# Expert gates: one-hot matrices of eight tokens by wide 16-bit tensor compares in place of one scalar compare per token

## The chip, the cores and the metric

One core of a Trainium2 chip runs the whole program. The metric is the device time of one launch in microseconds; the median of the runs shown is compared. PE is TensorE, PEld its weight loads, DVE is VectorE, ACT is ScalarE, POOL is GpSimd, SP the queue that issues the DMAs.

## The reference

Two stacked models of two layers each run over 256 tokens of width 1024. The change lies in the first model's expert layer, which both of its layers run:

```python
def peer_ffn(h, w_query, sub_keys, expert_u, expert_v):
    ...
    best_s, best_pos = lax.top_k(cand_s, PEER_TOPK)      # 8 heads, 16 experts of 16384 each
    idx = jnp.take_along_axis(cand_i, best_pos, axis=-1) # idx = i * 128 + j
    gate = jax.nn.softmax(best_s, axis=-1)
    ...
        act = jax.nn.gelu(jnp.einsum('cd,ced->ce', xc, u).astype(jnp.float32), approximate=False)
        return jnp.einsum('ce,ced->cd', (gc * act).astype(v.dtype), v)
```

Each token thus has 128 chosen experts, each with a gate, and its output is the sum over them of gate times gelu(x u) times v.

## The kernel before

The kernel gathers no expert. `peer` computes gelu(x u) for all 16384 experts and all tokens, and multiplies it by a dense matrix of gates that is zero where an expert wasn't chosen. The experts go in 128 chunks of 128: `uchunk(i)` takes a chunk of `uT` (512 KB by DMA), which `units` splits into a high and a low part (`whi` on ACT, L70; `wlo` by a subtraction on DVE, L74), and `sproj` forms x u by 24 matmuls of 256 columns (L96 to L98) into a PSUM bank of tag `f`. ACT applies gelu into the tile X (L451, L454). Three raw, three high and three low tiles let the loads run ahead; their instructions have a high priority.

The chosen experts come from `route(t)` on DVE (top-k, L459 to L500), which runs beside the first chunks. `softmax` is placed behind chunk EXP_AT and `slots` behind chunk IJ_AT; `slots` transposes the two halves i and j of each expert number and the gates, so that the 128 slots of a token lie on the partitions and the tokens along the free dimension (tiles IT, JT, WT).

`gates(tb, done)` then treats eight tokens at a time, 32 blocks per layer, one block behind every second chunk from GATE_AT on. For each token DVE compares the row 0 to 127 with the token's column of JT (tile B, one instruction, L531) and with its column of IT, times the gate's high and low 16-bit parts (tile A, two instructions, L533). PE multiplies B by both A's (L538, two matmuls of 128 columns per token), which sums over the slots into a 128 x 128 matrix of gates [j, i] per token, four tokens to a PSUM bank. For chunks that are already there, DVE multiplies X by the matrix (L545); for the later ones ACT copies it into X (L547), and the chunk's gelu goes to `gtmp` and is multiplied in by DVE (L452). Behind chunk 127, X is multiplied with the expert rows v (L109 to L113).

A scheduler orders each engine's instructions at build time by program order, priority and its own estimate of times; an engine then runs its list in order.

Of the kernel before, what the change touches and what calls it, by code (L numbers as in the profile page):

```python
# [12 lines left out]
F16 = mybir.dt.float16  # L13
# [3 lines left out]
ALU = mybir.AluOpType  # L17
# [4 lines left out]
S = 256  # L22
# [4 lines left out]
NEG = -1e30  # L27

PRIO = 1000
EXP_AT, IJ_AT, GATE_AT = 46, 52, 54  # L30
LN_PLAN = [(0, 1)] * 4 + [(0, 0), (1, 0), (0, 0), (0, 0), (1, 0), (0, 0)]
GSCALE = 32768.0
NCAND = [16 // (a + 1) for a in range(16)]
# [3 lines left out]
class Builder:  # L37
# [340 lines left out]
    def peer(self, l):  # L378
        nc, I, tc = self.nc, self.I, self.tc
# [2 lines left out]
        PX = px.enter_context(mk("px"))  # L382
        T = self.maker(PX)
        X = [T([128, 64, S], "X0"), None]
        io128 = T([128, 128], "io128", F16)
        nc.sync.dma_start(io128, I["c_io128"])
        JT = T([128, S], "JT")
        IT = T([128, S], "IT")
        WT = T([128, 2, S], "WT")
        T = self.maker(pr.enter_context(mk("pr", "right")))  # L390
        io50 = T([128, NC50], "io50")
        nc.sync.dma_start(io50, I["c_io50"])
# [18 lines left out]
        for t, p in enumerate(self.mblock(units)):  # L411
            q = T([128, 512], "qtok", bufs=2)
            nc.scalar.activation(q, p, AF.Copy)
            p = self.bank("t")
# [4 lines left out]
            p = self.bank()  # L419
# [6 lines left out]
        for hp, u in enumerate(units, 4):  # L426
            sk = sks[hp // 8]
            p = self.bank("f")
# [82 lines left out]
        def slots():  # L511

            for t in range(2):
                p = self.bank()
                for k in range(3):
                    tc.keep_in_program_order(nc.tensor.transpose(p[:, k * 128:(k + 1) * 128], ijws[t][:, k], self.ident))
                ts = slice(t * 128, (t + 1) * 128)
                nc.vector.tensor_copy(IT[:, ts], p[:, 0:128])
                nc.vector.tensor_copy(JT[:, ts], p[:, 128:256])
                nc.vector.tensor_scalar(WT[:, 0, ts], p[:, 256:384], GSCALE, None, ALU.mult)  # L520
                wh = T([128, 128], "wh16", F16, bufs=2)
                nc.vector.tensor_copy(wh, WT[:, 0, ts])
                nc.vector.tensor_sub(WT[:, 1, ts], WT[:, 0, ts], wh)

        def gates(tb, done):

            B = TG([128, 8, 128], "B", F16, bufs=2)
            A = TG([128, 8, 2, 128], "A", F16, bufs=2)
            for t in range(8):
                n = slice(tb * 8 + t, tb * 8 + t + 1)  # L530
                nc.vector.tensor_scalar(B[:, t], io128, JT[:, n], None, ALU.is_equal)  # L531
                for k in range(2):
                    nc.vector.tensor_scalar(A[:, t, k], io128, IT[:, n], WT[:, k, n], ALU.is_equal, ALU.mult)  # L533
            for q in range(2):
                p = self.bank("st"[q]).rearrange("p (t i) -> p t i", t=4)
                for t in range(4):
                    for k in range(2):
                        nc.tensor.matmul(p[:, t], B[:, q * 4 + t], A[:, q * 4 + t, k], start=(k == 0), stop=(k == 1))  # L538
                pv = p.rearrange("p t i -> p i t")
                ts = slice(tb * 8 + q * 4, tb * 8 + q * 4 + 4)  # L540
                for half in range(2):
                    n = min(max(done - half * 64, 0), 64)
                    o = half * 64
                    if n:
                        nc.vector.scalar_tensor_tensor(X[half][:, :n, ts], pv[:, o:o + n], 1.0 / GSCALE, X[half][:, :n, ts], ALU.mult, ALU.mult)  # L545
                    if n < 64:
                        nc.scalar.activation(X[half][:, n:, ts], pv[:, o + n:o + 64], AF.Copy, scale=1.0 / GSCALE)  # L547
            gated[0] = tb * 8 + 8
# [4 lines left out]
        for i in range(128):  # L553
            uchunk(i)
            if i == EXP_AT:
                softmax()
            if i == IJ_AT:
                slots()
                pr.close()
                X[1] = self.maker(p1.enter_context(mk("px1", "right")))([128, 64, S], "X1")  # L560
                TG = self.maker(pg.enter_context(mk("pg")))
            tb = (i - GATE_AT) // 2
            if i >= GATE_AT and (i - GATE_AT) % 2 == 0 and tb < 32:
                gates(tb, i + 1)
        pg.close()
        T = self.maker(px.enter_context(mk("pv")))
# [25 lines left out]
        T = self.maker(PL)  # L592
# [535 lines left out]
def pack_s(W):  # L1128
    d, c = W.shape
    return np.ascontiguousarray(W.reshape(d // 128, 128, c // 128, 128).transpose(2, 1, 0, 3)).reshape(c // 128, 128, d)  # L1130


def pack_m(W):
    r, c = W.shape
    q = 1024 // c
    return np.ascontiguousarray(W.reshape(r // (128 * q), q, 128, c).transpose(0, 2, 1, 3)).reshape(r // (128 * q), 128, 1024)
# [6 lines left out]
def bc(v):  # L1143
    return np.ascontiguousarray(np.broadcast_to(v, (128,) + v.shape))


def layout1(inp):
    A = {}
    x = inp["x"][0]
    A["xT"] = np.ascontiguousarray(x.T.reshape(8, 128, S).transpose(1, 0, 2))  # L1150
    A["x_tok"] = np.ascontiguousarray(x.reshape(2, 128, D).transpose(1, 0, 2))
    w = inp["w_in"]
    st = lambda f, *a: np.stack([f(*[v[l] for v in a]) for l in range(DEPTH)])

    def win(w):
        dq, dk, dv, sq, sk, sv = np.split(w, 6, axis=1)
        return np.concatenate([pack_m(dv), pack_s(np.concatenate([dq, dk, sq, sk], 1)), pack_m(sv)], 0)
    A["w_in"] = st(win, w)
    A["w_o"] = st(pack_m, inp["w_o"])
    A["w_query"] = st(pack_ms, inp["w_query"])  # L1160
    A["uT"] = st(lambda u: pack_s(u.T), inp["expert_u"])
    A["v"] = st(pack_m, inp["expert_v"])
    sk = inp["sub_keys"].reshape(DEPTH, 16, 128, 128)
    A["sub_keysT"] = np.ascontiguousarray(sk.reshape(DEPTH, 2, 8, 128, 128).transpose(0, 1, 4, 2, 3)).reshape(DEPTH, 2, 128, 1024)
    lam = np.stack([inp["lam_q1"], inp["lam_k1"], inp["lam_q2"], inp["lam_k2"]], 1)
    A["lam"] = np.ascontiguousarray(np.broadcast_to(lam[:, None], (DEPTH, 128, 4, 64)))
    A["subln_g"] = np.ascontiguousarray(np.broadcast_to(inp["subln_g"][:, None], (DEPTH, 128, 128)))
    gb = [(inp[f"ln{i}_g"][l], inp[f"ln{i}_b"][l]) for l in range(DEPTH) for i in (1, 2)]
    gb += [(inp["ln_g_2"][l, i], inp["ln_b_2"][l, i]) for l in range(DEPTH) for i in range(3)]
    gb = np.stack([np.stack(p) for p in gb])  # L1170
    A["ln_gb"] = np.ascontiguousarray(np.broadcast_to(gb[:, None], (10, 128, 2, D)))
    A["c_ident"] = np.eye(128, dtype=np.float32)
    q = np.arange(128)[:, None]
    s = np.arange(256)[None]
    dist = (128 + q - s).astype(np.float32)
    slopes = np.array([2.0 ** (-8.0 * (i + 1) / 4) for i in range(4)], np.float32)
    A["c_alibi"] = np.ascontiguousarray(np.where(dist[:, None] >= 0, -slopes[None, :, None] * dist[:, None], np.float32(NEG)).astype(np.float32))
    strict = (dist > 0).astype(np.float32)
    A["c_strict"] = np.ascontiguousarray(np.stack([strict, 1 - strict], 1))
    A["c_io128"] = bc(np.arange(128, dtype=np.float32)).astype(np.float16)  # L1180
    A["c_io50"] = bc(np.arange(NC50, dtype=np.float32))
    return A

# [97 lines left out]
```

## Time and profile before

| what | value |
|---|---|
| runs | 2992.4, 2996.71, 3002.91 us; median 2996.71 |
| profiled execution, its own time | 2998.15 us |
| its span, first to last instruction | 2996.3 us |
| mean granted TensorE clock, share of full speed | 0.983 |
| engine busy, share of the span | PE 96%, DVE 73%, ACT 49%, POOL 6% |

The profiled execution lies 1.4 us above the median. A timeline row tells an instruction's duration; instructions of one engine overlap at their ends, so what one costs its engine is read from the start of one to the start of the next. In a name, a digit at the end is left out: `io` is the tile io128 (or io50).

### The profile page before, as it was taken

Reading aid. Unit: us, or ns where it says so; the run is one execution under the profiler, and the core shown is the slowest. Engines: PE = TensorE matmul, PEld = TensorE weight load, DVE = VectorE, ACT = ScalarE, POOL = GpSimd, SP = SyncE. Lnnn points to the kernel's source line nnn. Section 1 sums busy time; section 2 is a strip of 40 time slices with the busy share of each in tenths; the row PEclk is TensorE's granted clock in tenths of the full one; section 3 lists DMA queues with packets and bytes.
Section 4 is the critical chain, followed back from the end, with each engine's and each line's share of the span. In section 5 each row is a group of like instructions: output and inputs, shape, how many; then the busy total and the mean of one; then the engine's idle time right before and its main releaser. Section 6 shows DMA issues by size and latency. Waiting matters only on the chain.

```text
span 2996.3 us, 51033 instructions
## 1 busy us (share of the span) xinstructions
PE 2876.5 (96%) x19030; PEld 2547.3 (85%) x19030; DVE 2193.6 (73%) x5317; ACT 1475.2 (49%) x2717; POOL 178.8 (6%) x134
## 2 busy tenths in 40 slices
PE   9999998899999989999999999999998999999898
PEld 8799988788888869998888888888886988888797
DVE  6699899966666678989996666666577647457665
ACT  5554544355555555444334555555544545454453
POOL 0320000000000024000000000000022000003100
PEclk9999999999999999999999999999999999899999
DMA  6456543366666535654445667663344555235354
GB/s 211 149 173 201 156 135 121 119 184 196 207 194 200 179 114 170 192 168 134 127 121 162 193 202 226 193 195 111 110 155 130 191 194 173 96 111 172 132 187 160
DMA packets 139337, 489.89 MB, mean 163 GB/s; under 512 B 17024, under 2 KB 22224, under 8 KB 137680
## 3 DMA queue, kind: packets, MB, share of 16 engines
q1 hardware_dynamic: 139088, 486.62, 51.7%
q8 instruction: 150, 2.46, 0.3%
q14 instruction: 99, 0.81, 0.1%
HBM read 484.97 MB, written 1.06 MB: 162 GB/s over the span
## 4 chain that ended last, share of the span: by engine, by line
PE 77%; DVE 17%; issue 3%; ACT 2%; DMA 1%; POOL 0%; DVEq 0%; SPq 0%; ACTq 0%; POOLq 0%
PE f L96 12%; PE f L97 11%; PE f L98 11%; PE acc L109 5%; PE acc L113 5%; PE acc L111 5%; DVE A L533 5%; DVE wlo L74 4%; PE s L111 4%; PE s L109 4%; PE s L113 4%; DVE B L531 2%; DVE X L545 1%; PE f L109 1%; PE f L111 1%
## 5 line engine op out<-in xcount | busy, mean ns | idle before, releaser
L70 ACT ACTIVATE whi<-raw 128x1024 fp32r<-128x1024 f32 x874 | 925.8, 1060 | 896.9 <-PE f L97 426.1
L74 DVE TENSOR_TENSOR wlo<-raw,whi 128x1024 fp32r<-128x1024 f32 x832 | 1028.6, 1238 | 461.4 <-ACT whi L70 457.6
L96 PE MATMUL f<-xh,whi 128*128 128x256 f32 x3600 | 1045.3, 290 | 44.3 <-ACT X L454 33.5
L97 PE MATMUL f<-xl,whi 128*128 128x256 f32 x3600 | 1035.1, 288 | 0.8 <-DVE xl L74 0.8
L98 PE MATMUL f<-xh,wlo 128*128 128x256 f32 x3600 | 1034.0, 287 | 0.0
L96 PEld LDWEIGHTS f<-xh,whi 128*128 128x128 f32 x3600 | 692.3, 192 | 67.0 <-ACT X L454 46.9
L98 PEld LDWEIGHTS f<-xh,wlo 128*128 128x128 f32 x3600 | 693.2, 193 | 6.2 <-issue 5.0
L97 PEld LDWEIGHTS f<-xl,whi 128*128 128x128 f32 x3600 | 691.7, 192 | 6.8 <-issue 4.4
L533 DVE TENSOR_SCALAR A<-io,IT,WT 128x128 f16<-128x128 f16 x1024 | 284.9, 320 | 0.0
L70 ACT ACTIVATE Hh<-X 128x256 fp32r<-128x256 f32 x249 | 104.0, 418 | 177.8 <-PE s L111 177.5
L74 DVE TENSOR_TENSOR Hl<-X,Hh 128x256 fp32r<-128x256 f32 x249 | 105.6, 425 | 111.7 <-PE s L113 110.6
L109 PE MATMUL acc<-whi,Hh 128*128 128x512 f32 x498 | 153.5, 390 | 3.2 <-ACT Hh L70 3.2
L109 PE MATMUL s<-whi,Hh 128*128 128x512 f32 x498 | 153.9, 390 | 0.0
L113 PE MATMUL s<-whi,Hl 128*128 128x512 f32 x498 | 153.9, 390 | 0.0
L113 PE MATMUL acc<-whi,Hl 128*128 128x512 f32 x498 | 153.7, 390 | 0.0
L111 PE MATMUL s<-wlo,Hh 128*128 128x512 f32 x498 | 153.7, 389 | 0.0
L111 PE MATMUL acc<-wlo,Hh 128*128 128x512 f32 x498 | 153.3, 389 | 0.0
L531 DVE TENSOR_SCALAR B<-io,JT 128x128 f16<-128x128 f16 x512 | 132.9, 260 | 0.0
L109 PEld LDWEIGHTS acc<-whi,Hh 128*128 128x128 f32 x498 | 93.3, 188 | 23.1 <-ACT Hh L70 3.6
L538 PEld LDWEIGHTS <-B 128*128 128x128 f16 x1024 | 77.7, 97 | 41.3 <-DVE B L531 6.3
L111 PEld LDWEIGHTS s<-wlo,Hh 128*128 128x128 f32 x498 | 93.5, 188 | 20.2 <-issue 0.9
L113 PEld LDWEIGHTS acc<-whi,Hl 128*128 128x128 f32 x498 | 93.5, 188 | 19.8 <-issue 0.5
(474 smaller groups left out, 3937.6 us busy)
## 6 DMA issues: line engine op xcount, KB each, us to landing
raw<-uT SPq DMA_DIRECT2D x256, 512.0 KB, 3.7
raw<-v SPq DMA_DIRECT2D x256, 512.0 KB, 3.6
raw<-w_in SPq DMA_DIRECT2D x90, 512.0 KB, 4.0
raw<-w_up SPq DMA_DIRECT2D x64, 512.0 KB, 3.8
raw<-w_down SPq DMA_DIRECT2D x64, 512.0 KB, 4.3
raw<-w_gate SPq DMA_DIRECT2D x48, 512.0 KB, 3.7
raw<-w_query SPq DMA_DIRECT2D x32, 512.0 KB, 3.8
gb<-ln_gb SPq DMA_DIRECT2D x10, 1024.0 KB, 6.4
```

The lines of the kernel that those rows point to most:

```text
L70: nc.scalar.activation(hi, raw, AF.Copy)
L74: (nc.vector if eng == "V" else nc.gpsimd).tensor_sub(lo, raw, hi.bitcast(F32))
L96: mm(out, hi[:, w], xh[:, k], start=(k == 0), stop=False)
L97: mm(out, hi[:, w], xl[:, k], start=False, stop=False)
L98: mm(out, lo[:, w], xh[:, k], start=False, stop=(k == nk - 1))
L109: mm(accs[t][n], a, hi[:, n * 512:(n + 1) * 512], start=start, stop=False)
L111: mm(accs[t][n], a, lo[:, n * 512:(n + 1) * 512], start=False, stop=False)
L113: mm(accs[t][n], b, hi[:, n * 512:(n + 1) * 512], start=False, stop=stop)
L531: nc.vector.tensor_scalar(B[:, t], io128, JT[:, n], None, ALU.is_equal)
L533: nc.vector.tensor_scalar(A[:, t, k], io128, IT[:, n], WT[:, k, n], ALU.is_equal, ALU.mult)
L538: nc.tensor.matmul(p[:, t], B[:, q * 4 + t], A[:, q * 4 + t, k], start=(k == 0), stop=(k == 1))
L545: nc.vector.scalar_tensor_tensor(X[half][:, :n, ts], pv[:, o:o + n], 1.0 / GSCALE, X[half][:, :n, ts], ALU.mult, ALU.mult)
```

## The change

B, and A without its weights, are each made by one compare of eight tokens (`tensor_tensor`, 1024 elements per partition, all 16-bit). The tokens lie in pairs: the innermost dimension of each operand is the two tokens of a pair, next to each other, the middle one the 128 values of i or j, the outer one the four pairs. The constant row is held with each number twice (`io2`); a token's column of IT or JT is read with a step of 0 over the 128 values. Two wide products then give the high and the low weighted A (tile A3). JT, IT and WT become 16-bit; `slots` keeps its number of instructions. The gate matmuls keep their number and size; both their operands now have a step of two elements. B and A3 have two buffers, A has one. The three placement constants move: EXP_AT from 46 to 45, IJ_AT from 52 to 50, GATE_AT from 54 to 52.

```diff
--- before.py
+++ after.py
@@ -27,7 +27,7 @@
 NEG = -1e30
 
 PRIO = 1000
-EXP_AT, IJ_AT, GATE_AT = 46, 52, 54
+EXP_AT, IJ_AT, GATE_AT = 45, 50, 52
 LN_PLAN = [(0, 1)] * 4 + [(0, 0), (1, 0), (0, 0), (0, 0), (1, 0), (0, 0)]
 GSCALE = 32768.0
 NCAND = [16 // (a + 1) for a in range(16)]
@@ -382,11 +382,11 @@
         PX = px.enter_context(mk("px"))
         T = self.maker(PX)
         X = [T([128, 64, S], "X0"), None]
-        io128 = T([128, 128], "io128", F16)
-        nc.sync.dma_start(io128, I["c_io128"])
-        JT = T([128, S], "JT")
-        IT = T([128, S], "IT")
-        WT = T([128, 2, S], "WT")
+        io2 = T([128, 128, 2], "io2", F16)
+        nc.sync.dma_start(io2, I["c_io2"])
+        JT = T([128, S], "JT", F16)
+        IT = T([128, S], "IT", F16)
+        WT = T([128, 2, S], "WT", F16)
         T = self.maker(pr.enter_context(mk("pr", "right")))
         io50 = T([128, NC50], "io50")
         nc.sync.dma_start(io50, I["c_io50"])
@@ -517,25 +517,29 @@
                 ts = slice(t * 128, (t + 1) * 128)
                 nc.vector.tensor_copy(IT[:, ts], p[:, 0:128])
                 nc.vector.tensor_copy(JT[:, ts], p[:, 128:256])
-                nc.vector.tensor_scalar(WT[:, 0, ts], p[:, 256:384], GSCALE, None, ALU.mult)
-                wh = T([128, 128], "wh16", F16, bufs=2)
-                nc.vector.tensor_copy(wh, WT[:, 0, ts])
-                nc.vector.tensor_sub(WT[:, 1, ts], WT[:, 0, ts], wh)
+                wr = T([128, 128], "wr", bufs=2)
+                nc.vector.tensor_scalar(wr, p[:, 256:384], GSCALE, None, ALU.mult)
+                nc.vector.tensor_copy(WT[:, 0, ts], wr)
+                nc.vector.tensor_sub(WT[:, 1, ts], wr, WT[:, 0, ts])
 
         def gates(tb, done):
 
-            B = TG([128, 8, 128], "B", F16, bufs=2)
-            A = TG([128, 8, 2, 128], "A", F16, bufs=2)
-            for t in range(8):
-                n = slice(tb * 8 + t, tb * 8 + t + 1)
-                nc.vector.tensor_scalar(B[:, t], io128, JT[:, n], None, ALU.is_equal)
-                for k in range(2):
-                    nc.vector.tensor_scalar(A[:, t, k], io128, IT[:, n], WT[:, k, n], ALU.is_equal, ALU.mult)
+            n8 = slice(tb * 8, tb * 8 + 8)
+            pairs = lambda x: x.rearrange("p (g t) -> p g t", t=2)[:, :, None, :].broadcast_to([128, 4, 128, 2])
+            io = io2[:, None].broadcast_to([128, 4, 128, 2])
+            B = TG([128, 4, 128, 2], "B", F16, bufs=2)
+            A = TG([128, 4, 128, 2], "A", F16)
+            A3 = TG([128, 2, 4, 128, 2], "A3", F16, bufs=2)
+            nc.vector.tensor_tensor(B, io, pairs(JT[:, n8]), ALU.is_equal)
+            nc.vector.tensor_tensor(A, io, pairs(IT[:, n8]), ALU.is_equal)
+            for k in range(2):
+                nc.vector.tensor_mul(A3[:, k], A, pairs(WT[:, k, n8]))
             for q in range(2):
                 p = self.bank("st"[q]).rearrange("p (t i) -> p t i", t=4)
                 for t in range(4):
+                    g = (q * 4 + t) // 2
                     for k in range(2):
-                        nc.tensor.matmul(p[:, t], B[:, q * 4 + t], A[:, q * 4 + t, k], start=(k == 0), stop=(k == 1))
+                        nc.tensor.matmul(p[:, t], B[:, g, :, t % 2], A3[:, k, g, :, t % 2], start=(k == 0), stop=(k == 1))
                 pv = p.rearrange("p t i -> p i t")
                 ts = slice(tb * 8 + q * 4, tb * 8 + q * 4 + 4)
                 for half in range(2):
@@ -1177,7 +1181,7 @@
     A["c_alibi"] = np.ascontiguousarray(np.where(dist[:, None] >= 0, -slopes[None, :, None] * dist[:, None], np.float32(NEG)).astype(np.float32))
     strict = (dist > 0).astype(np.float32)
     A["c_strict"] = np.ascontiguousarray(np.stack([strict, 1 - strict], 1))
-    A["c_io128"] = bc(np.arange(128, dtype=np.float32)).astype(np.float16)
+    A["c_io2"] = bc(np.repeat(np.arange(128, dtype=np.float32)[:, None], 2, axis=1)).astype(np.float16)
     A["c_io50"] = bc(np.arange(NC50, dtype=np.float32))
     return A
```

## Rows read from the trace of the kernel before

**Rows 1.** The page, part 1: busy time of each engine and its share.
```profile
PE 2876.5 (96%) x19030; PEld 2547.3 (85%) x19030; DVE 2193.6 (73%) x5317; ACT 1475.2 (49%) x2717; POOL 178.8 (6%) x134
```

**Rows 2.** Windows: start:end, length, then busy us and count of each engine, clock, DMA.
```profile
187.00:331.70 144.70, 143.93 (x1267) 143.53 (x1266) 133.30 (x371) 74.98 (x112) 0.00 (x0) 1.00 0.63 191
331.70:604.90 273.20, 247.93 (x2091) 228.92 (x2091) 273.20 (x1019) 109.31 (x265) 0.00 (x0) 0.98 0.41 126
...
1318.60:1594.00 275.40, 251.28 (x2107) 232.62 (x2106) 275.40 (x1020) 109.86 (x268) 0.00 (x0) 0.96 0.42 127
```

**Rows 3.** Timeline of DVE within a block of eight tokens: start, duration.
```profile
444.56 0.27 DVE L531 TENSOR_SCALAR B<-io,JT 128x128 f16<-128x128 f16 x1
444.72 0.56 DVE L533 TENSOR_SCALAR A<-io,IT,WT 128x128 f16<-128x128 f16 x2
445.17 0.28 DVE L531 TENSOR_SCALAR B<-io,JT 128x128 f16<-128x128 f16 x1
```

**Rows 4.** Waits from 332 to 605 us: total us, times, longest.
```profile
ACT X L547 <- DVE X L545: 51.9, 34, 3.7
...
PE f L96 <- ACT X L454: 19.1, 17, 2.2
```

**Rows 5.** Timeline of DVE behind the last block of the first layer.
```profile
612.22 1.23 DVE L74 TENSOR_TENSOR wlo<-raw,whi 128x1024 fp32r<-128x1024 f32 x1 [1.16 <-ACT whi L70]
613.36 0.42 DVE L452 TENSOR_TENSOR X<-X,gtmp 128x256 f32<-128x256 f32 x1
614.94 1.23 DVE L74 TENSOR_TENSOR wlo<-raw,whi 128x1024 fp32r<-128x1024 f32 x1 [1.16 <-ACT whi L70]
```

**Rows 6.** Timeline of PE: chunk matmuls alone.
```profile
628.03 0.28 PE L96 MATMUL f<-xh,whi 128*128 128x256 f32 x1
...
628.26 0.28 PE L98 MATMUL f<-xh,wlo 128*128 128x256 f32 x1
```

**Rows 7.** Timeline of PE: one gate matmul between chunk matmuls.
```profile
447.77 0.28 PE L96 MATMUL f<-xh,whi 128*128 128x256 f32 x1
447.90 0.23 PE L538 MATMUL t<-A,B 128*128 128x128 f16 x1
...
448.14 0.28 PE L98 MATMUL f<-xh,wlo 128*128 128x256 f32 x1
```

**Rows 8.** Timeline of PE: a run of six gate matmuls.
```profile
440.66 0.51 PE L538 MATMUL t<-A,B 128*128 128x128 f16 x6
```

**Rows 9.** Groups by line and shape: count, busy us, mean ns of one.
```profile
L98 PEld LDWEIGHTS f<-xh,wlo 128*128 128x128 f32 x3600 | 693.2, 193 | 6.2 <-issue 5.0 <-DVE wlo L74 0.2
...
L74 DVE TENSOR_TENSOR wlo<-raw,whi 128x1024 fp32r<-128x1024 f32 x832 | 1028.6, 1238 | 461.4 <-ACT whi L70 457.6 <-DMA tri<-c_tri 0.6
...
L538 PEld LDWEIGHTS <-B 128*128 128x128 f16 x1024 | 77.7, 97 | 41.3 <-DVE B L531 6.3 <-DVE A L533 6.0 <-issue 3.5
...
L187 DVE SCALAR_TENSOR_TENSOR ln_r<-ln_r,ln_mv,gb 128x512 f32<-128x512 f32 x40 | 40.5, 1042 | 1.4 <-ACT h L178 1.4
...
L487 DVE TENSOR_TENSOR eq<-io,u 128x400 f32<-128x400 f32 x64 | 34.9, 566 | 0.1
...
L623 DVE TENSOR_SCALAR sma<-sma,za 128x256 f32<-128x256 f32 x64 | 19.6, 349 | 0.8
...
L623 DVE TENSOR_SCALAR sma<-sma,za 128x128 f32<-128x128 f32 x48 | 11.4, 281 | 0.3
```

**Rows 10.** Timeline of DVE at the end of the routing, first layer.
```profile
310.46 0.22 DVE L492 CAST u<-sel 128x128 int32<-128x128 f32 x1
310.71 0.23 DVE L494 TENSOR_SCALAR ij<-u 128x128 int32<-128x128 int32 x1
310.86 0.22 DVE L495 TENSOR_SCALAR ij<-u 128x128 int32<-128x128 int32 x1
311.11 0.29 DVE L497 CAST ijw<-ij 128x256 f32<-128x256 int32 x1
```

**Rows 11.** Timeline of ACT at the softmax of the gates, first layer.
```profile
315.01 1.28 ACT L503 ACT_TABLE_LOAD   x1
```


## Prediction

> **What bounds the kernel now.** I read the page first: PE is busy 96% of the span and DVE 73% [rows 1], so a change on DVE can only pay in a stretch where DVE sets the pace. The windows by stage show one. While the first 55 chunks of a layer run without gates, PE is busy 143.9 of 144.7 us and DVE 133.3; from the first gate compare to the last (64 chunks, 32 blocks of eight tokens) DVE is busy all of 273.2 us in the first layer and all of 275.4 in the second, while PE has 25 us with nothing in flight and ACT is busy for less than half [rows 2]. So DVE bounds 548.6 us of the launch, and PE the chunks on both sides.
>
> The timeline of DVE says how much of that is the one-hots: a compare for B costs 0.16 us from its start to the next, the two for A 0.45, together 0.61 per token [rows 3]. That is 256 x 0.607 = 155 us per layer; what is left of the stage, 273.2 - 155 = 118 us, is the splits of the chunks and the gating of X, and is not touched (120 us in the second layer). The waits inside the stage show what a late DVE does: ACT stood 51.9 us behind DVE's gating of X, and PE 19.1 us until ACT had emptied a chunk's bank [rows 4].
>
> **What PE needs.** Behind the last block a chunk takes 614.94 - 612.22 = 2.72 us, and DVE is idle 1.16 us of it [rows 5]; three chunk matmuls take two steps of 0.115 us from 628.03 to 628.26 [rows 6]. Sixty-four chunks are 174 us. With one gate matmul in between, the same two steps take 0.37 us [rows 7], so a lone one costs 0.14 us; in a run of six each further one costs (0.51 - 0.23)/5 = 0.056 us [rows 7, 8]. A block's 16 in one run cost 0.14 + 15 x 0.056 = 0.98 us, 31 us per layer; all alone, 72 us. PE's own need is thus 205 to 246 us per layer. Now A becomes ready token by token, and I saw most gate matmuls alone; with the change all 16 of a block become ready at its last product, and they stand ahead of the later chunks in program order, so I take 205.
>
> **The wide compare and product.** Gone per block are 24 short DVE instructions, 4.86 us; in come four of 1024 elements. No 16-bit two-source instruction is in the trace, so their price is bounded. Above: the 32-bit two-source form of 1024 elements costs 613.36 - 612.22 = 1.14 us [rows 5]. Its slope against the form of 400 elements is (1238 - 566)/624 = 1.08 ns per element [rows 9], so some 0.03 to 0.05 us of it is fixed. Below: a one-source 32-bit form runs at (349 - 281)/128 = 0.53 ns per element [rows 9], and a 16-bit one at no more than about 0.4: B's 0.16 us, less the 0.06 that A's second pointer scalar adds to it, less 0.05 fixed, over 128 elements [rows 3], an estimate. 1024 x 0.4 + 0.05 gives 0.46 us. I take 0.60 us: in one-source form the 16-bit data ran faster than the 32-bit data, and half of 1.08 ns is the like step for two sources. The first product waits for the compare of A on its own engine; such a wait adds 0.10 us (0.25 from 310.46 to 310.71, where the next, independent one starts 0.15 later [rows 10]), 3 us per layer. B's compare and the second product wait for nothing new. DVE's sum per layer: 118 + 128 x 0.60 + 3 = 198 us (180 at 0.46, 267 at 1.14).
>
> The Trainium skill, Vector Engine (DVE) Microarchitecture Reference, section 5.1 (Performance modes), says that a two-source operation takes two elements per cycle when all operands are 16-bit with an innermost step of one and more than one element in that dimension, which a pair fulfils. By that rule and the 0.96 GHz it gives, a wide instruction would stream for 0.53 us, an estimate near the value taken; no run here shows it yet.
>
> **Which engine then ends last.** 198 us on DVE lie under 205 on PE: the stage becomes PE's. What the compares don't hide any more is the chunk matmuls themselves, so further DVE savings would be worth nothing. The two engines feed each other through ACT, and PE's waits of 19.1 us [rows 4] need not go to zero with DVE 96% as busy as PE; against that stand the chunks before the gates, where DVE at 92% cost PE under 1 us [rows 2]. I add 13 us, between 0 and 25. The granted clock was 0.98 and 0.96 in the gated stages and 1.00 before them [rows 2]; at 0.97 PE's 205 would be 211, inside that term. Stage: 205 + 13 = 218 us in each layer.
>
> **What costs nothing.** PE issues the same 512 gate matmuls, at a step of two 16-bit elements, 4 bytes: the chunk matmuls read 4-byte elements at 0.115 us per 256 columns, 0.45 ns each, against 0.056/128 = 0.44 ns in the run of gate matmuls [rows 6, 8], so the moving side is covered; the weights are a rival below. `slots` keeps five DVE instructions per half. The constant grows from 32 to 64 KB per layer, one load on SP at the head of the expert layer; its first reader comes over 140 us after the first chunk [rows 2], and without that cover it would delay the loads behind it by less than one 512 KB chunk, 2.7 us. The placement moves the gated stretch two chunks forward without adding to it: 53 plain chunks before and 13 behind in place of 55 and 11. Its softmax moves a chunk forward, to 315.01 - 2.72 = 312.3 us [rows 11], still behind the routing's last instruction at 311.11 + 0.29 [rows 10]; if routing slipped by over a microsecond there, only the slots, four chunks later, would be due next. A has one buffer, but only DVE touches it, in order; B and A3 have two, so DVE can run a block ahead of PE.
>
> **Sum.** (273.2 - 218) + (275.4 - 218) = 55 + 57 = 112 us off the profiled execution's 2998.15: 2886 us (3.7% under the median of 2996.71, from which the profiled one differs by 1.4 us). With no friction 2860; with 25 us of it and runs of eight gate matmuls (3 us more per layer) 2916.
>
> **Rivals.**
> 1. PE pays for the strided weights. The 16-bit load takes 97 ns, the 32-bit one 193 [rows 9]; if a step of two elements brings it to the 32-bit pace, a gate matmul costs 0.115 in place of 0.056: 174 + 32 x (0.14 + 15 x 0.115) + 13 = 247 us, gain 26 + 29, 2943 us. Gate matmuls that stay scattered end at the same place (246 + some wait). For it: nothing shows a strided 16-bit load; against: the load overlaps the matmul before.
> 2. The four-byte pieces of the token columns slow the stream. One two-source row runs at 1042 ns for 512 elements [rows 9], 1.52 times what the slope gives (566 + 112 x 1.08 = 687); it belongs to the layer norm, where GpSimd works beside DVE; in the gated stage GpSimd does nothing [rows 2]. On the value taken that is 1024 x 0.54 x 1.52 + 0.05 = 0.89 us, DVE 118 + 114 + 3 = 235, with 13 us 248: 2945 us. Against: the compare of L487 reads one word 50 times over and keeps the slope. [...]
> 3. No gain of rate from 16 bits: 1.14 us each, DVE 267, DVE bound as now: gain 6 + 6, 2986 us.
> 4. The other side: no gain of rate and the pieces slow it too. 1024 x 1.08 x 1.52 + 0.05 = 1.73 us, DVE 118 + 221 + 3 = 342, 69 + 67 us longer, 3134 us. It decides from 155/128 less the wait, 1.19 us per instruction, where the profile's nearest form has 1.14.
> 5. DVE gets faster and the stage stays: PE's list has a block's 16 matmuls ahead of a chunk and waits for the whole chain of four (2.5 us) where it now waits for a token. It needs 68 us, 2.1 us in every block; double-buffered B and A3 speak against it. 2997 us.
>
> **Chances.** Forecast 0.57, rival 1 0.15, rival 2 0.11, rival 3 0.07, rival 4 0.06, rival 5 0.04. Range 2858 to 2950, which takes in the forecast and rivals 1 and 2 (0.83). A measurement here tells about 0.3% (9 us) from nothing: forecast, rivals 1 and 2 and most of rival 3 are faster, 0.88; rival 5 and some of rival 3 the same, 0.06; rival 4 slower, 0.06.
>
> **What would show it.** In the trace after: four DVE rows of 128x1024 16-bit at 0.6 us from start to start (1.14: rival 3; 0.9: rival 2), DVE no longer busy all the time between the first and the last gate compare, PE's waits for ACT's emptying down, weight loads of gate matmuls at about 97 ns in runs of 16 at 0.056 us (193 ns and 0.115: rival 1), and a stage of 218 us. The prediction is wrong if the wide rows take over 1.19 us, or if they take 0.6 and the stage still is above 245 us.

## The result, and the profile after

The changed kernel takes 2884.11 us (median of four runs, 2883.76 to 2888.77). The kernel before, run beside it on the same chip, takes 2994.56 (2986.37 to 3002.91). The ratio is 0.9635, 95% interval 0.9605 to 0.9664. The forecast was 2886 us. The profiled execution takes 2884.09 us, 114.06 less than the profiled one of before.

The page, part 1, of the changed kernel, against [rows 1]:

```profile
PE 2814.0 (98%) x19030; PEld 2517.7 (87%) x19030; DVE 2047.5 (71%) x4037; ACT 1465.3 (51%) x2721; POOL 179.2 (6%) x134
```

DVE has 1280 instructions fewer and PE the same number, but DVE's share fell by only 2 points. The share hides the change: what matters is where DVE was busy. The windows from the first compare for B to the last gating of X, one for each layer, answer to the gated windows of [rows 2], with the same columns:

```profile
327.05:540.11 213.06, 213.06 (x2058) 211.56 (x2057) 198.81 (x375) 102.83 (x265) 0.00 (x0) 1.00 0.52 160
1261.27:1474.32 213.05, 213.05 (x2058) 211.54 (x2057) 198.82 (x375) 102.82 (x265) 0.00 (x0) 1.00 0.52 160
```

Cut at the same instructions, the stretches before take 274.76 us (from 332.25) and 275.92 us (from 1319.10); the windows of [rows 2] end 2 and 1 us ahead of the last gating. The roles are exchanged. Before, DVE was busy in all of the stretch and PE had 25 us with nothing in flight; now PE is busy in all of it and DVE is free for 14 us. The timeline of DVE in a block answers to [rows 3]:

```profile
421.00 0.68 DVE L536 TENSOR_TENSOR A<-A,WT 128x1024 f16<-128x1024 f16 x1
421.60 0.21 DVE L549 SCALAR_TENSOR_TENSOR X<-s,X 128x60 f32<-128x60 f32 x1
...
425.12 0.68 DVE L533 TENSOR_TENSOR B<-io,JT 128x1024 f16<-128x1024 f16 x1
425.72 1.22 DVE L74 TENSOR_TENSOR wlo<-raw,whi 128x1024 fp32r<-128x1024 f32 x1
```

A wide product and a wide compare each take 0.60 us from their start to the next start. The 32-bit split of the same 1024 elements still takes 1.14 [rows 5]. PE's timeline, against [rows 7, 8]:

```profile
430.17 0.28 PE L98 MATMUL f<-xh,wlo 128*128 128x256 f32 x1
430.29 0.63 PE L542 MATMUL s<-A,B 128*128 128x128 f16 x8
430.77 0.62 PE L542 MATMUL t<-A,B 128*128 128x128 f16 x8
431.19 0.36 PE L96 MATMUL f<-xh,whi 128*128 128x256 f32 x1
431.40 0.28 PE L97 MATMUL f<-xl,whi 128*128 128x256 f32 x1
```

All 16 gate matmuls of this block stand together, eight into each bank, with no chunk matmul between them; so do those of every block but the first two, which stand as two and fourteen. The weight load by form, and the waits of the first gated stretch:

```profile
L542 PEld LDWEIGHTS <-B 128*128 128x128 f16 x512 | 29.4, 97 | 1.5
```

```profile
ACT whi L70 <- PE f L97: 106.1, 62, 2.5
DVE X L549 <- PE s L542: 9.1, 20, 0.8
DVE wlo L74 <- ACT whi L70: 2.0, 2, 1.4
ACT X L551 <- DVE X L549: 1.9, 1, 1.9
```

The load takes 97 ns at a step of two elements, as it did packed [rows 9]. ACT's 51.9 us behind DVE's gating [rows 4] are 1.9 now, PE's 19.1 us for a bank are gone, and nearly all that is left is waiting for PE.

**Where the time came from.** The chunks of the first product end where ACT makes the last of their splits; a gap of 4.7 us to the next split follows in every run. The split 82 chunks ahead of it stands before the gates. In the changed kernel these are, for the first layer and for the second, these rows of ACT's timeline:

```profile
310.59 1.06 ACT L70 ACTIVATE whi<-raw 128x1024 fp32r<-128x1024 f32 x1 [1.39 <-PE f L97]
...
574.34 1.06 ACT L70 ACTIVATE whi<-raw 128x1024 fp32r<-128x1024 f32 x1 [1.50 <-PE f L97]
...
1244.80 1.06 ACT L70 ACTIVATE whi<-raw 128x1024 fp32r<-128x1024 f32 x1 [1.50 <-PE f L97]
...
1508.56 1.06 ACT L70 ACTIVATE whi<-raw 128x1024 fp32r<-128x1024 f32 x1 [1.50 <-PE f L97]
```

The same four splits of before, with one more that is used below:

```profile
310.94 1.06 ACT L70 ACTIVATE whi<-raw 128x1024 fp32r<-128x1024 f32 x1 [1.39 <-PE f L97]
...
630.16 1.06 ACT L70 ACTIVATE whi<-raw 128x1024 fp32r<-128x1024 f32 x1 [1.39 <-PE f L97]
...
1297.68 1.06 ACT L70 ACTIVATE whi<-raw 128x1024 fp32r<-128x1024 f32 x1 [1.50 <-PE f L97]
...
1300.51 1.06 ACT L70 ACTIVATE whi<-raw 128x1024 fp32r<-128x1024 f32 x1 [1.50 <-PE f L97]
...
1618.78 1.06 ACT L70 ACTIVATE whi<-raw 128x1024 fp32r<-128x1024 f32 x1 [1.39 <-PE f L97]
```

I call the time from the first to the second of these splits, and from the third to the fourth, the gated part of a layer. It went from 319.2 to 263.8 us in the first layer and from 321.1 to 263.8 in the second, so the two gave 55.5 and 57.3 us. Between the two parts 2.9 us were lost and behind them 3.8 gained; these are not explained here.

**The pace of the chunks.** One thing in the trace after is not in the prediction. ACT's splits follow PE chunk by chunk, so their starts show PE's pace. Before the gates of the first layer, within a block, and behind the last block:

```profile
291.55 1.06 ACT L70 ACTIVATE whi<-raw 128x1024 fp32r<-128x1024 f32 x1 [1.39 <-PE f L97]
294.27 1.07 ACT L70 ACTIVATE whi<-raw 128x1024 fp32r<-128x1024 f32 x1 [1.39 <-PE f L97]
...
427.54 1.06 ACT L70 ACTIVATE whi<-raw 128x1024 fp32r<-128x1024 f32 x1 [2.42 <-PE f L97]
430.37 1.06 ACT L70 ACTIVATE whi<-raw 128x1024 fp32r<-128x1024 f32 x1 [1.00 <-PE f L97]
434.18 1.06 ACT L70 ACTIVATE whi<-raw 128x1024 fp32r<-128x1024 f32 x1 [2.42 <-PE f L97]
...
546.08 1.06 ACT L70 ACTIVATE whi<-raw 128x1024 fp32r<-128x1024 f32 x1 [1.50 <-PE f L97]
548.90 1.06 ACT L70 ACTIVATE whi<-raw 128x1024 fp32r<-128x1024 f32 x1 [1.50 <-PE f L97]
```

A chunk takes 2.72 us before the gates and 2.83 behind them, where no gate matmul is left. With its 24 matmuls that is 0.113 and 0.118 us for one. The granted clock is 1.00, the 2.4 GHz level, in both gated windows, and PE is busy without a break. Within the gates, a chunk takes 2.83 us and the next one with a block behind it 3.81, so a block costs 0.98 us, as forecast, and each chunk 0.11 us more than forecast. The slow pace could have been read before the change: in the second layer of before, ahead of any gate, the splits at 1297.68 and 1300.51 stand 2.83 us apart, while [rows 5, 6] are from the first layer.

### The profile page after: what moved, and what is told of

It reads as the page before. It is cut to its first block, busy times and chain, and to the rows that moved or that the text cites. A ratio compares the mean times of both kernels' runs of the same rounds, so it can differ in the third digit from the quotient of the medians.

```text
span 2882.3 us, 49733 instructions
## 1 busy us (share of the span) xinstructions
PE 2814.0 (98%) x19030; PEld 2517.7 (87%) x19030; DVE 2047.5 (71%) x4037; ACT 1465.3 (51%) x2721; POOL 179.2 (6%) x134
## 4 chain that ended last, share of the span: by engine, by line
PE 85%; DVE 9%; issue 2%; DMA 2%; ACT 1%; POOL 0%; DVEq 0%; ACTq 0%; POOLq 0%
PE f L96 14%; PE f L98 13%; PE f L97 13%; PE acc L109 5%; PE acc L113 5%; PE acc L111 5%; PE s L111 4%; PE s L113 4%; PE s L109 4%; DVE wlo L74 2%; PE s L542 1%; PE t L542 1%; PE f L109 1%; PE f L111 1%; PE s L809 1%
## 5 line engine op out<-in xcount | busy, mean ns | idle before, releaser
L96 PE MATMUL f<-xh,whi 128*128 128x256 f32 x3600 | 1023.5, 284 | 8.2 <-ACT xh L70 6.1
L97 PE MATMUL f<-xl,whi 128*128 128x256 f32 x3600 | 1012.8, 281 | 0.8 <-DVE xl L74 0.8
L98 PE MATMUL f<-xh,wlo 128*128 128x256 f32 x3600 | 1012.2, 281 | 0.0
L96 PEld LDWEIGHTS f<-xh,whi 128*128 128x128 f32 x3600 | 679.8, 189 | 19.4 <-ACT xh L70 6.1
L97 PEld LDWEIGHTS f<-xl,whi 128*128 128x128 f32 x3600 | 684.4, 190 | 6.7 <-issue 4.5
L98 PEld LDWEIGHTS f<-xh,wlo 128*128 128x128 f32 x3600 | 681.1, 189 | 4.4 <-issue 3.2
L113 PEld LDWEIGHTS s<-whi,Hl 128*128 128x128 f32 x498 | 93.5, 188 | 19.7 <-issue 0.2
L109 PEld LDWEIGHTS s<-whi,Hh 128*128 128x128 f32 x498 | 93.5, 188 | 19.6 <-issue 0.2
L111 PEld LDWEIGHTS acc<-wlo,Hh 128*128 128x128 f32 x498 | 93.5, 188 | 19.4
```

What stands on the lines that cost most here:

```text
L96: mm(out, hi[:, w], xh[:, k], start=(k == 0), stop=False)
L97: mm(out, hi[:, w], xl[:, k], start=False, stop=False)
L98: mm(out, lo[:, w], xh[:, k], start=False, stop=(k == nk - 1))
L109: mm(accs[t][n], a, hi[:, n * 512:(n + 1) * 512], start=start, stop=False)
L111: mm(accs[t][n], a, lo[:, n * 512:(n + 1) * 512], start=False, stop=False)
L113: mm(accs[t][n], b, hi[:, n * 512:(n + 1) * 512], start=False, stop=stop)
```

## The experiments

My theory: in the gated stretch the longer of DVE's and PE's own work sets the time; the wide operations at 0.60 us brought DVE under PE; the rate comes from the pair layout; the placement is worth nothing. Rivals: the placement or the single product carries part of the gain; DVE still limits; the order of the gate matmuls matters and not the rate of DVE. Later a second question came up, what sets the two paces. Each kernel was timed beside the kernel before on its own chip; ratios are to that.

**The placement.** Two runs: the changed kernel with the old placement, and the kernel before with the new one.

```diff
-EXP_AT, IJ_AT, GATE_AT = 45, 50, 52
+EXP_AT, IJ_AT, GATE_AT = 46, 52, 54
```

The second run makes the reverse edit to the kernel before.

> The changed kernel with the three placement constants put back (46, 52, 54). Main theory: in the gated stage the slower of DVE and PE sets the time; the wide 16-bit compares took DVE from 273 to about 200 us, under PE's 212, and the placement is worth nothing: 2884 us, within 3. Rival, placement: starting the gates two chunks earlier carries part of the 110 us, then this run is above 2893 us.

> The kernel before with the three new placement constants and nothing else. Main theory: DVE still needs 273 us for the gated stage wherever it lies, so 2995 us, within 9. Rival, placement: under 2985 us.

The first took 2885.15 us (2883.65 to 2888.2), ratio 0.9618 (0.9588 to 0.9648); the second 3005.9 (2994.36 to 3014.03) against 2997.76, ratio 1.003 (1.001 to 1.005). The first is as expected. The second is 2 us over the range given for it, and away from its rival, which asked for under 2985. The placement is worth nothing in the new kernel, and in the old one it does not help.

**Wide, but without the pairs.** The same four operations, with the tokens laid out one after the other; the value of a token is then broadcast along the innermost dimension, and the gate matmuls read packed operands.

```diff
-pairs = lambda x: x.rearrange("p (g t) -> p g t", t=2)[:, :, None, :].broadcast_to([128, 4, 128, 2])
-B = TG([128, 4, 128, 2], "B", F16, bufs=2)
+pairs = lambda x: x[:, :, None].broadcast_to([128, 8, 128])
...
+B = TG([128, 8, 128], "B", F16, bufs=2)
...
-nc.tensor.matmul(p[:, t], B[:, g, :, t % 2], A3[:, k, g, :, t % 2], start=(k == 0), stop=(k == 1))
+nc.tensor.matmul(p[:, t], B[:, q * 4 + t], A3[:, k, q * 4 + t], start=(k == 0), stop=(k == 1))
```

> The changed kernel with the same four wide 16-bit instructions per block, but token by token: the token's column is read with a step of 0 in the innermost dimension and the constant row is held once, so the matmul operands are contiguous again. Main theory: what pays is the rate, and the pairs give it; without pairs an instruction takes 1.1 us or more, DVE's sum is 118 + 128 x 1.14 + 3 = 267 us per layer and DVE bounds again: 2984 us (2970 to 2995). Rival, count: 4 instructions in place of 24 are what pays, or any wide 16-bit form has the doubled rate: 2884 us. Rival, PE runs: PE's runs of gate matmuls are what pays; they stay, so under 2920 us.

It took 2973.03 us (2964.21 to 2985.81), ratio 0.9913 (0.9886 to 0.9939). Its timeline of DVE:

```profile
422.92 1.22 DVE L534 TENSOR_TENSOR A<-io,IT 128x1024 f16<-128x1024 f16 x1
424.05 1.22 DVE L74 TENSOR_TENSOR wlo<-raw,whi 128x1024 fp32r<-128x1024 f32 x1
...
427.20 2.36 DVE L536 TENSOR_TENSOR A<-A,WT 128x1024 f16<-128x1024 f16 x2
```

The compare takes 1.13 us to the next start, the price of the 32-bit split. So 16 bits alone give no rate, and fewer instructions alone give under 1%: this is the state that rival 3 of the prediction describes. The 89 us between this run and the changed kernel (83 by the ratios) belong to the pairs.

**One half of the change.** B by the wide compare, A token by token as before.

```diff
-nc.vector.tensor_tensor(A, io, pairs(IT[:, n8]), ALU.is_equal)
-for k in range(2):
-    nc.vector.tensor_mul(A3[:, k], A, pairs(WT[:, k, n8]))
+for t in range(8):
+    n = slice(tb * 8 + t, tb * 8 + t + 1)
+    for k in range(2):
+        nc.vector.tensor_scalar(A3[:, t, k], io128, IT[:, n], WT[:, k, n], ALU.is_equal, ALU.mult)
...
```

> One part alone: B by one wide paired compare, A by 16 scalar compares per block as before. Main theory: DVE loses 8 x 0.16 - 0.60 = 0.7 us per block, 22 us per layer, and stays the bound at 251 us: 2884 + (251 - 214) x 2 = 2958 us (2945 to 2970). Rival, PE runs: the gate matmuls stay scattered because A comes token by token, so no gain, 2995 us. Rival, all or nothing (a new wait for whole blocks eats the saving): over 2980 us.

It took 2966.57 us (2962.76 to 2969.09), ratio 0.9885 (0.9854 to 0.9916): in the range, 9 us above its middle. DVE was busy for 254.34 of the 259.60 us from 332.28 to 591.88 and still bound the stretch. B's saving was paid for the most part, not in full: DVE's busy time fell by 20.4 us against the stretch of before, and the gated parts are 13.5 and 15.4 us shorter, of the 22 that the expectation took. PE stood 23.1 us of this stretch waiting for ACT to empty a bank.

**DVE given less than it has now.** The low product is left out; both matmuls of a token read the high one.

```diff
...
-for k in range(2):
-    nc.vector.tensor_mul(A3[:, k], A, pairs(WT[:, k, n8]))
+nc.vector.tensor_mul(A3[:, 0], A, pairs(WT[:, 0, n8]))
...
-A3[:, k, g, :, t % 2]
+A3[:, 0, g, :, t % 2]
```

> The changed kernel without the product for the low parts of the gates; both gate matmuls of a token read the high product, so PE's work is the same and DVE has one wide instruction (0.60 us) less per block. Main theory: PE is now the bound (busy all 214 us of the stage, DVE with gaps), so nothing is won: 2884 us, within 4. Rival, DVE still co-bounds: 32 x 0.6 = 19 us per layer less, 2846 us.

It took 2892.08 us (2887.97 to 2893.96), ratio 0.9638 (0.9612 to 0.9663). The window from its first compare for B to its last gating:

```profile
327.33:540.42 213.09, 213.09 (x2057) 211.68 (x2057) 181.07 (x343) 103.28 (x265) 0.00 (x0) 1.00 0.53 160
```

DVE has 17.7 us less to do and the stretch is as long as before, 213.09 against 213.06. In the second layer it is 213.10. The whole is 8 us above the changed kernel, outside the expected 4, but not in what the edit touches: the last split of the second layer stands at 1509.45, 0.9 us behind the changed kernel's, and the rest arises behind it. There, from 2400 to 2570 us, the granted clock was 0.93 in this run and 0.98 in the changed kernel's. The rival's 2846 is out.

**PE given less.** Eight of a block's 16 gate matmuls, the low ones, are left out; DVE does all it did.

```diff
-for k in range(2):
-    nc.tensor.matmul(p[:, t], B[:, g, :, t % 2], A3[:, k, g, :, t % 2], start=(k == 0), stop=(k == 1))
+nc.tensor.matmul(p[:, t], B[:, g, :, t % 2], A3[:, 0, g, :, t % 2], start=True, stop=True)
```

> The changed kernel without the gate matmuls of the low parts (8 of 16 per block); DVE makes both products as before. Main theory: PE bounds, so each of the 8 gives back its 0.056 us: 0.45 x 32 x 2 = 29 us, and DVE's 200 us lie just above PE's new 198, so 2855 to 2865 us. Rival, DVE co-bounds: 2884 us, unchanged.

It took 2859.97 us (2855.13 to 2871.76), ratio 0.9547 (0.9516 to 0.9578). The window:

```profile
327.47:535.15 207.68, 202.78 (x1838) 200.52 (x1838) 197.41 (x377) 106.24 (x269) 0.00 (x0) 1.00 0.54 167
```

Less PE work is paid, and only until DVE is nearly full again: 197.41 us busy of 207.68. Two chunks and a block take 3.35 + 2.83 us where DVE keeps up, and five times a chunk waits (a step of 4.4 in place of 3.36):

```profile
PE f L96 <- ACT X L454: 4.9, 5, 1.1
```

The whole is in the expected range, but the gated parts gave 9.4 us each, not the 14.3 of 256 matmuls at 0.056; the other 5 of the 24 us lie outside them, so the hit is in part luck.

**DVE given more.** The compare for A is made three times, and in a later run twice.

```diff
-nc.vector.tensor_tensor(A, io, pairs(IT[:, n8]), ALU.is_equal)
+for _ in range(3):    # range(2) in the later run
+    nc.vector.tensor_tensor(A, io, pairs(IT[:, n8]), ALU.is_equal)
```

> The changed kernel with the compare for A made three times over (two more wide instructions per block, 1.2 us). Main theory: DVE's sum rises from 200 to 238 us per layer and bounds the stage again: 2884 + 2 x (238 - 214) = 2932 us, up to 15 more if waits add. Rival, the stage has slack on DVE beyond that or waits set it: under 2900 us.

> The comparison for A is made twice for each block (one repeated), which adds one wide operation of 0.60 us to DVE and changes nothing else. If a stage is as long as the longer of DVE and PE: the run with two repeats stands 59 us above the changed kernel, 29.5 us per stage, so its stage is about 213.6 + 29.5 = 243 us; one repeat less is 32 x 0.60 = 19.3 us less, 224 us, so the time is 2884 + 2 x 10 = 2904 (2893 to 2910). If every operation that DVE is given costs its own time, 2884 + 2 x 19.3 = 2923. If DVE still has room, 2884.

They took 2943.19 us (2938.28 to 2950.12), ratio 0.9819 (0.9791 to 0.9846), and 2898.81 (2893.86 to 2901.63), ratio 0.9676 (0.9647 to 0.9705), both as expected. The windows of the one and of the other:

```profile
326.90:572.41 245.51, 222.43 (x2089) 216.34 (x2089) 237.60 (x440) 109.47 (x267) 0.00 (x0) 0.99 0.48 141
```

```profile
326.54:554.00 227.46, 220.48 (x2090) 217.45 (x2090) 217.51 (x408) 107.59 (x267) 0.00 (x0) 0.98 0.51 153
```

From none to one to two repeats DVE's busy time goes up by 18.7 and 20.1 us, the stretch by 14.4 and 18.1. Each longer stretch also takes in chunk matmuls that stood behind it before, 32 with the first repeat; the gated part of the first layer grows by 10.5 and 18.2 us, that of the second by 9.3 and 19.1. The first repeat is paid in part, the second nearly in full: the two engines cross between. Near the crossing the stretch is longer than the busy time of its busier engine: by 7.0 us with one repeat (PE), by 7.9 with two (DVE), and by 4.9 in the run with half the matmuls (PE).

**The gate matmuls spread out.** Pairs of them are handed in between the chunk matmuls of the next chunk.

```diff
-self.sproj(next(uit), p[:, :S])
+self.sproj(next(uit), p[:, :S], between=between)
...
+def between(t):
+    if t % 4 == 0:
+        ps.append(self.bank("st"[t // 4]).rearrange("p (t i) -> p t i", t=4))
+    for k in range(2):
+        nc.tensor.matmul(ps[-1][:, t % 4], B[:, t // 2, :, t % 2], A3[:, k, t // 2, :, t % 2], start=(k == 0), stop=(k == 1))
...
```

> The changed kernel with a block's 16 gate matmuls spread over the next chunk, two behind each group of three chunk matmuls, in place of one run; DVE's work is the same. Main theory: PE bounds and a change between the two kinds of matmul costs it 0.08 us; 8 pairs cost 8 x 0.19 = 1.52 us in place of 0.98 per block, 34 us in all: 2918 us (2905 to 2930). Rival, the order on PE is free: 2884 us.

It took 2899.86 us (2896.34 to 2903.78), ratio 0.9669 (0.9643 to 0.9696): 16 us lost, half of the 34 expected. Its PE timeline in a block:

```profile
430.79 0.57 PE L543 MATMUL s<-A,B 128*128 128x128 f16 x7
...
432.64 0.23 PE L543 MATMUL s<-A,B 128*128 128x128 f16 x1
...
433.12 0.29 PE L543 MATMUL t<-A,B 128*128 128x128 f16 x2
...
435.04 0.28 PE L97 MATMUL f<-xl,whi 128*128 128x256 f32 x1
...
437.42 0.28 PE L97 MATMUL f<-xl,whi 128*128 128x256 f32 x1
```

Seven still stood together, one stood alone and four pairs followed: six entries in a block in place of one. Two chunks and a block take 6.87 us in place of 6.64, 0.23 x 64 = 15 us. Behind the last pair, 21 steps take 437.42 - 435.04 = 2.38 us, 0.113 each: there PE is back at the fast pace, which gave part of the loss back. The gated parts, with the fast chunks behind the last block, are 6.4 us longer each, 13 us in all; the rest lies outside them. That led to the question of the paces.

**What sets the pace.** Three runs change the run of gate matmuls itself: 15 in a block (one low matmul left out), eight behind each chunk, and 17 in a block (one high product multiplied twice).

```diff
 for k in range(2):
+    if k and q * 4 + t == 7:
+        continue
-    nc.tensor.matmul(..., start=(k == 0), stop=(k == 1))
+    nc.tensor.matmul(..., start=(k == 0), stop=(k == 1 or q * 4 + t == 7))
```

> The low product of the eighth token of a block is left out of the gate matmuls, so a block has 15 of them in place of 16; VectorE does what it did. Left out of the computation: the low part of one weight in eight. 32 x 0.056 = 1.8 us less of PE per layer, so 2880 (2876 to 2884) if that is all. The rival: that the chunk matmuls behind a gate run keep the slow pace of 2.83 us a chunk because a run has an even number of matmuls, and an odd run turns the pace over; then every second block runs at 2.72, 64 x 0.055 = 3.5 us less again per layer, 2873 or lower, and the starts of whi stand 2.72 apart in some blocks.

```diff
-if i >= GATE_AT and (i - GATE_AT) % 2 == 0 and tb < 32:
-    gates(tb, i + 1)
+if i >= GATE_AT and tb < 32:
+    gates(tb, i + 1, (i - GATE_AT) % 2)    # the half q of the block's matmuls and gating
...
-gated[0] = tb * 8 + 8
+gated[0] = tb * 8 + 4 + q * 4
...
```

> The 16 gate matmuls of a block are issued 8 after its first chunk and 8 after its second, with the gating of each half behind them; the wide operations and the totals are the same. A lone gate matmul cost 0.14 us against 0.056 in a run [rows 7, 8], so entering a run costs some 0.085 us; 32 more runs per layer add 2.7 us, and the time is 2884 + 2 x 2.7 = 2889 (2884 to 2895). The rival: that shorter runs let the chunk matmuls keep the pace of 2.72 us; then 2 x 7 us come off and the time is about 2875.

```diff
 for t in range(4):
     g = (q * 4 + t) // 2
+    if q * 4 + t == 7:
+        nc.tensor.matmul(p[:, t], B[:, g, :, 1], A3[:, 0, g, :, 1], start=True, stop=True)
     for k in range(2):
```

> The first product of a block's eighth token is multiplied twice (the second time over the first result), so a block has 17 gate matmuls, an odd number, and one more than the changed kernel, where the run with 15 had one fewer. Nothing is left out. If it was the odd number that held the chunk matmuls at 2.72 us: two chunks and a block take the 6.38 us of the run with 15 and two matmuls of 0.056 us, 6.49 in place of 6.64, 32 x 0.15 = 4.8 us less per layer, and the chunks behind the last block come 2.72 apart (some 10 x 0.11 = 1 us per layer): 2884 - 12 = 2872 (2866 to 2877). If it was that the run was shorter, the pace stays at 2.83 and the matmuls are 2 x 32 x 0.056 = 3.6 us more: 2888 (2884 to 2893).

| gate matmuls in a run | us, median (range) | ratio (95%) | two chunks and a block, us | split of the last chunk, first layer, against 574.34 |
|---|---|---|---|---|
| 16 (the change) | 2884.11 (2883.76 to 2888.77) | 0.9635 (0.9605 to 0.9664) | 3.81 + 2.83 | |
| 15 | 2863.2 (2860.06 to 2871.28) | 0.9558 (0.9524 to 0.9591) | 3.66 + 2.72 | 566.96, 7.4 earlier |
| 8 and 8 | 2895.24 (2882.49 to 2899.2) | 0.9654 (0.9615 to 0.9693) | 3.36 + 3.35 | 576.21, 1.9 later |
| 17 | 2875.26 (2869.32 to 2882.74) | 0.9603 (0.9583 to 0.9623) | 3.79 + 2.72 | 569.21, 5.1 earlier |

ACT's splits, of the run with 15 and of the run with 17:

```profile
428.15 1.06 ACT L70 ACTIVATE whi<-raw 128x1024 fp32r<-128x1024 f32 x1 [0.90 <-PE f L97]
...
431.81 1.06 ACT L70 ACTIVATE whi<-raw 128x1024 fp32r<-128x1024 f32 x1 [2.27 <-PE f L97]
...
434.53 1.06 ACT L70 ACTIVATE whi<-raw 128x1024 fp32r<-128x1024 f32 x1 [0.91 <-PE f L97]
```

```profile
428.67 1.06 ACT L70 ACTIVATE whi<-raw 128x1024 fp32r<-128x1024 f32 x1 [0.89 <-PE f L97]
...
432.46 1.06 ACT L70 ACTIVATE whi<-raw 128x1024 fp32r<-128x1024 f32 x1 [2.40 <-PE f L97]
...
435.18 1.06 ACT L70 ACTIVATE whi<-raw 128x1024 fp32r<-128x1024 f32 x1 [0.91 <-PE f L97]
```

With 15 and with 17 in a run the chunks keep 2.72 us, in the gates and behind them; with 16 and with eight they take 2.83 (3.355 is 2.83 and 0.53, that is eight times 0.056 and 0.08 for the entry). The gated parts of both layers are 8.5 us shorter with 15, of which the left-out matmul is 1.8, 5.1 shorter with 17 and 2.3 longer with eight and eight. It is not that the run is shorter, since 17 is longer. My rival had the odd run turn the pace over in every second block; it is fast in every block, and the run with 15 came out 10 us under that rival's 2873. The run with eight and eight is just over its range of 2884 to 2895; its two gated parts cost 4.7 us, near the 5.4 expected, and the rest arises outside them.

The run with the old placement shows the turn within one kernel. From the third block on PE ran 16 in a row, at the slow pace; only the last block stands as one and fifteen, and the chunks behind it are fast, in both layers:

```profile
539.28 0.23 PE L542 MATMUL s<-A,B 128*128 128x128 f16 x1
...
541.91 0.58 PE L542 MATMUL s<-A,B 128*128 128x128 f16 x7
...
542.33 0.62 PE L542 MATMUL t<-A,B 128*128 128x128 f16 x8
```

```profile
548.38 1.06 ACT L70 ACTIVATE whi<-raw 128x1024 fp32r<-128x1024 f32 x1 [1.39 <-PE f L97]
...
551.10 1.06 ACT L70 ACTIVATE whi<-raw 128x1024 fp32r<-128x1024 f32 x1 [1.39 <-PE f L97]
```

Odd or even is not the whole rule, since behind the last pair in the run with the matmuls spread out the pace was fast too. Nor do the gate matmuls alone decide it. Ahead of the gates the programs are alike, and there both paces occur: the slow one in the first layer of two runs (B alone wide, and the matmuls spread out) and in the second layer of five (before, the change, one product, three compares, and 15 in a run), the fast one in the other 21 of the 28 layers profiled. What in PE holds these paces is not settled.

The version with 17 leaves nothing out and is the best found: 9 us under the changed kernel by the medians. The two intervals of the ratio overlap, but the gated parts, 5.1 us shorter in both layers, show where its gain lies. By the end of the second layer its last split is 13.9 us earlier (1494.70 against 1508.56); the other 3.6 us arise between the gated parts, where this run has the fast pace ahead of the gates and the changed kernel the slow one. The run with 15 has the slow one there too, so I do not count them for the edit.

## Why the prediction was right, point by point

**DVE bound the gated stretch, and the one-hots were what it could lose.** Right. Adding DVE work back makes the time rise again, and the half change gave 13.5 and 15.4 us of the some 20 that DVE was spared in a layer.

**The wide operation at 0.60 us.** Right to the digit shown: 0.60 from start to start for compares and products; the four-byte pieces cost nothing that shows. DVE's sum was 198 us, its measured busy time 198.81. Rivals 2 to 4 fall with it. The factor of 1.52 in rivals 2 and 4 was a misreading of a mean: of the 40 rows of L187 behind the 1042 ns, 34 take 734 to 752 ns, 1.08 times what the slope gives; six take 2564 to 2825 ns, and in each of them a GpSimd instruction of some 2.4 to 2.8 us runs at the same time.

The Trainium skill, Vector Engine (DVE) Microarchitecture Reference, section 5.1 (Performance modes), asks for 16-bit operands and more than one element at step one in the innermost dimension for two elements per cycle. The trace agrees on both sides: 0.60 us with the pairs, where the estimate by its rate was 0.53 of streaming, and 1.13 us in the run whose innermost step is zero.

**PE's own need, 205 us.** Right in the gate matmuls (0.98 us per block, loads at 97 ns, so rival 1 falls), short in the chunks: 64 were taken at 2.72 us, the pace of [rows 5], and took 2.83, the pace of the second layer's plain chunks in the same trace, 64 x 0.11 = 7 us more. 64 x 2.83 + 32 x 0.98 = 212.5, and the stretch is 213.06.

**The friction of 13 us.** Mis-sized, and of another kind. I took it for waits between two nearly equal engines. There are none on PE in the stretch: it is busy for all of its 213 us. What stood in its place is the 7 us of the slower pace, most of which the run with 17 takes back: 209.28 us in its window from 327.04 to 536.32, where it issues 32 gate matmuls more. Friction of the kind I meant is there once DVE's load comes nearer: 5 to 8 us in the runs with repeats and with half the matmuls.

**The stage, 218 us, and the gain, 55 + 57.** The stretch is 213 us, 5 shorter than forecast, and 61.7 and 62.9 us shorter than the same stretch before, but the gated parts gave only 55.5 and 57.3 us. The lengths of the windows don't subtract cleanly: the one of before ended on DVE, with PE already ahead, and held 2102 matmuls in the first layer where the one after holds 2058, that is 44 x 0.113 = 5.0 us of chunks which now come behind the gates; in the second layer 2112, 6.1 us. And the 13 chunks behind the last block run at 2.83 us, 13 x 0.11 = 1.4 us. That accounts for the 6.2 us of the first layer and for more than the 5.6 of the second. Counted from the windows of [rows 2], 273.2 and 275.4 us, the subtraction gives 4.6 and 5.0 us too much, and the stage in it was forecast 5 us too long. The mechanism was right; that the gain came out within 0.5 us of 55 and 57, and the whole within 2, is luck.

**What costs nothing.** Right for the placement, by its own two runs. The constant's load and DVE's wait for its own compare show nowhere in the list of waits.

**Further DVE savings would be worth nothing.** Right: 17.7 us less DVE work left the stretch at 213.09.

**Rival 5, PE waiting for the chain of four.** It falls: no wait of PE is left in the stretch.

**Scattered gate matmuls.** The price of an entry was 0.14 - 0.056 = 0.085 us; the expectation of 34 us for that run counted more entries than were made, and took the chunk pace as fixed.

## What to carry to other kernels

When an engine off the average bound is at 100% in one stretch, price its removal only down to the next engine's own need there, and give that engine work or take it away to find the crossing. For 16-bit two-source work on VectorE, look at the innermost dimension first: pairs made the same 1024 elements cost 0.60 us in place of 1.13. A pace read in one stretch of a stream need not hold in another; read it in every layer, and behind the pattern that the change will make, if the trace has one. And compare two runs between the same two instructions: the whole times here also hold up to 9 us from stretches that the edits leave alone.

## What the runs showed of the hardware

A steady stream of the 32-bit chunk matmuls (256 columns, a weight load of 128 columns for each) has two paces at a granted clock of 1.00: 0.113 us and 0.118 us per matmul, 4% apart, without idle time in either. It keeps the one it is in over ten chunks and more. Where PE never waited, runs of 16 or eight 16-bit matmuls between the chunks left it at the slow one, runs of 15 or 17 at the fast one; a single repeated matmul per block, 32 x 0.056 = 1.8 us a layer, came with a gated part 5.1 us shorter. Ahead of any gate matmul both paces occur in like programs, so something else decides there; the cause is open. Also not expected: a 16-bit weight load at a step of two elements takes the 97 ns of a packed one, and entering a run of 16-bit matmuls costs some 0.08 to 0.12 us, for one matmul as for 17.
